# Reading split weights behind the first differential head's operands, and cutting GpSimd's two-tile operations into pieces of 256 columns

## The chip, the cores and the metric

The kernel runs on one core of a Trainium2 chip. The metric is the time of one execution on the device in microseconds (us); less is better. A core has TensorE (matmuls; PE in the profile), VectorE (DVE), ScalarE (ACT), GpSimd (POOL) and SyncE (SP), which issues all of this kernel's DMAs on one queue.

## The reference

Two layers of a decoder trunk on one sequence of 512 tokens, 1024 wide, in float32. Per layer: a half-step SwiGLU network, a mixer of three head groups, another half-step network. Cut to what matters here:

```python
for l in range(DEPTH):                                   # DEPTH = 2
    x = x + 0.5 * swiglu(rmsnorm(x, ffn1_norm[l]), ffn1_wg[l], ffn1_wu[l], ffn1_wd[l])
    h = rmsnorm(x, mix_norm[l]) @ w_in[l]                # one projection for all three groups
    h_a, h_b, h_c = jnp.split(h, [A_COLS, A_COLS + B_COLS], axis=-1)
    o_a = mla_mixer(h_a, ...)                            # 6 heads
    o_b = nsa_mixer(h_b, ...)                            # 6 heads: compressed, selected and window branches
    o_c = diff_mixer(h_c, ...)                           # 4 differential heads
    x = x + jnp.concatenate([o_a, o_b, o_c], axis=-1) @ w_out[l]
    x = x + 0.5 * swiglu(rmsnorm(x, ffn2_norm[l]), ffn2_wg[l], ffn2_wu[l], ffn2_wd[l])
return rmsnorm(x, final_norm)
```

A differential head computes two causal softmax attentions with q and k of 32 columns each and subtracts one, times a learned factor, from the other. Some columns of q and k are turned by position (rotary embedding) first.

## The kernel before

**Arithmetic.** Products are made as three passes over split numbers: each float32 operand becomes a high part (rounded on ScalarE, L162) and a low part (the difference, L164, on VectorE or GpSimd; L166 where a scale comes in). `split` makes such a pair, `mm3` and `mm3y` run the passes (0,0), (0,1), (1,0) for each k tile of 128. `SPARE` names the places whose low part GpSimd makes. Weights go through `weights`: a DMA to a `raw` tile (4 buffers), then the split into a `whl` tile of 1 MB (4 buffers).

**Split ahead.** `AHEAD` names eight column blocks of w_in. During the first network's down projection `split_ahead` splits these and stores the 1 MB pair in a DRAM array, `pre`. When the mixer comes to such a block, `weights` finds its key in `PRE` and reads the pair back (L185, `whl<-pre`) in one DMA on SyncE's queue.

**The start of the mixer.** `project2` makes column blocks 12 and 13 (q and k of the differential heads are blocks 12 to 15), `project` 14 and 15. `c_done` rotates, scales and splits each and `put` writes each half into one of two DRAM arrays, `S["C"]` (`part<-b`, L755, eight writes of 256 KB). `c_load(h)` gathers the operands of head h from them in six DMAs of 128 KB (`qk<-part`, L194). `c_load(0)` comes next, then `norm_token`, then the value projection of this group.

**Periods.** From there `PLAN` sets the order. A row names the head whose scores are made (front), the head whose weighted sum is made (back), an order string, and the items whose matmuls `period` puts between them. The first row is `("c0", "", "...f.f..f.f..f..f..", "p2 p0 cl1 cl2")`: the scores of differential head 0 with the projections of blocks 2 and 0 and the loads for heads 1 and 2. The second has head 1's scores, head 0's weighted sum, and `"lat p1 b3 cl3 an"`. `p2`, `p0`, `p1` call `project`; block 2 is `AHEAD[0]`. TensorE's order is fixed by the program there (`mm` keeps it); on the other engines a scheduler that simulates the program places each instruction. SyncE's DMAs share eight completion semaphores in turn, so an issue waits for the landing of the eighth DMA before it.

**GpSimd.** It does L164 where asked, both multiplications and the last of `rsqrt_slow` (L211, L212, L214), the second half of each rotation (L556, L557 in `rope`, L729, L730 in `roped`, L952, L953 in `a_query`) and L866, besides the squares of the norms (L298) and a few more. Up to here each of them is one instruction, over 192 to 1024 columns.

Of the kernel before, what the change touches and what calls it, by code (L numbers as in the profile page):

```python
# [14 lines left out]
ALU = mybir.AluOpType  # L15
AX = mybir.AxisListType

P = 128
# [74 lines left out]
SPARE = ('an', 'h6', 'h9', 'ho3', 'ho4', 'hq0', 'hq1', 'hq2', 'hq3', 'w0', 'w2', 'w3', 'w7')  # L93
NROW = 2

AHEAD = (2, 0, 1, 3, 9, 8, 5, 4)
# [7 lines left out]
def tile_hybrid_trunk(ctx: ExitStack, tc: tile.TileContext, I, out, dbg=None):  # L104
    nc = tc.nc
    pe, ve, sc, gp, sy = nc.tensor, nc.vector, nc.scalar, nc.gpsimd, nc.sync
# [11 lines left out]
    def nm(s):  # L118
        uid[0] += 1
        return f"{s}_{uid[0]}"  # L120
# [5 lines left out]
    def psum(tags, shape=(P, T)):  # L126
        turn[0] += 1
        tag = tags[turn[0] % len(tags)]
        return pp.tile(list(shape), F32, tag=tag, name=nm("ps" + tag), bufs=BANKS[tag])
# [6 lines left out]
    def pair(tag, dt=F32R):  # L136
        return bp.tile([P, 2, T], dt, tag=tag, name=nm(tag), bufs=PAIRS[tag])

    def tmp(dt=F32, shape=(P, T)):
        return tp.tile(list(shape), dt, tag="t", name=nm("t"), bufs=6)  # L140
# [8 lines left out]
    def loaded(src):  # L149
        t = tp.tile([P, T], F32, tag="xin", name=nm("xin"), bufs=2)  # L150
        sy.dma_start(t, src)
        return t
# [4 lines left out]
    def f32(ap):  # L157
        return ap.bitcast(F32) if ap.dtype == F32R else ap

    def split(src, hi, lo, scale=None, eng=ve):  # L160

        high = sc.copy(hi, src) if scale is None else sc.mul(hi, src, scale)  # L162
        if scale is None:
            eng.tensor_tensor(lo, src, f32(hi), op=ALU.subtract)  # L164
        else:
            eng.scalar_tensor_tensor(lo, src, scale, f32(hi), op0=ALU.mult, op1=ALU.subtract)  # L166
        return high

    def weight_tiles():
        return (wp.tile([P, 8 * P], F32, tag="raw", name=nm("raw"), bufs=RAWS),  # L170
                wp.tile([P, 2, WPAD], F32R, tag="whl", name=nm("whl"), bufs=WHLS))

    PRE = {}

    def split_ahead(src, key):

        hl = weights(src, eng=ve)
        d = PRE[key] = dp.tile([P, 2, 8 * P], F32, name=nm("pre"))
        sy.dma_start(d, f32(hl[:, :, :8 * P]))

    def weights(src, rows=P, cols=8 * P, eng=gp, key=None):

        if key in PRE:
            hl = wp.tile([P, 2, WPAD], F32R, tag="whl", name=nm("whl"), bufs=WHLS)
            sy.dma_start(f32(hl[:, :, :8 * P]), PRE.pop(key))  # L185
            return hl
        raw, hl = weight_tiles()
        sy.dma_start(raw[:rows, :cols], src)
        split(raw[:rows, :cols], hl[:rows, 0, :cols], hl[:rows, 1, :cols], eng=eng)
        return hl  # L190

    def move(dst, src):

        return sy.dma_start(f32(dst), f32(src))  # L194

    PASS = ((0, 0), (0, 1), (1, 0))
# [8 lines left out]
    def rsqrt_slow(ps, mul, r):  # L205

        ms, y = tmp(), tmp()
        sc.activation(y, ps, AF.Ln, bias=epst, scale=mul)
        sc.activation(ms, ps, AF.Identity, bias=epst, scale=mul)
        sc.activation(y, y, AF.Exp, scale=-0.5)  # L210
        gp.tensor_tensor(r, y, y, op=ALU.mult)  # L211
        gp.tensor_tensor(r, r, ms, op=ALU.mult)  # L212
        sc.activation(r, r, AF.Identity, bias=halft, scale=-0.5)
        gp.tensor_tensor(r, r, y, op=ALU.mult)  # L214
        return r

    def rsqrt(ps, mul, r):
# [117 lines left out]
    tabs = dp.tile([3, 2, P, T], F32, name="tabs")  # L335
# [29 lines left out]
    def halves_of(src):  # L365

        n = src.shape[1]
        hl = wp.tile([P, 2, WPAD], F32R, tag="whl", name=nm("whl"), bufs=WHLS)
        split(src, hl[:, 0, :n], hl[:, 1, :n])
        return hl  # L370
# [180 lines left out]
    def rope(src, cos, sin, swap, r0=0, r1=P, eng=gp):  # L551

        t, sw = tmp()[r0:r1], tmp()[r0:r1]
        ve.stream_shuffle(sw, src, swap)
        ve.tensor_tensor(t, src, cos[r0:r1], op=ALU.mult)
        eng.tensor_tensor(sw, sw, sin[r0:r1], op=ALU.mult)  # L556
        eng.tensor_tensor(t, t, sw, op=ALU.add)  # L557
        return t

    def mm(*args, **kw):  # L560
# [3 lines left out]
    def mm3y(ps, pairs):  # L564

        n = len(pairs)
        for k, (w, x) in enumerate(pairs):
            for j, (a, b) in enumerate(PASS):
                mm(ps, w(a), x(b), start=k == j == 0, stop=k == n - 1 and j == 2)
                yield  # L570
# [101 lines left out]
    def mix(l, xn, nxt):  # L672
# [4 lines left out]
        S = {}  # L677
# [15 lines left out]

        def project(c, done, eng=gp):

            w = weights(I["w_in"][l, c], eng=ve if "w%d" % c in SPARE else eng, key=("in", l, c))
            pj = psum("m")
            yield from mm3y(pj, [((lambda a, k=k: w[:, a, k * P:(k + 1) * P]), (lambda b, k=k: xg[k][:, b])) for k in range(KD)])
            done(pj)
# [18 lines left out]
        def scaled(pj, by):  # L718
            t = tmp()
            ve.tensor_tensor(t, pj, by, op=ALU.mult)  # L720
            return t

        def roped(pj, g, swap, n=P, eng=gp):

            t = scaled(pj, rs[0])
            c, sw = tmp()[:n], tmp()[:n]
            ve.stream_shuffle(sw, t[:n], swap)
            ve.tensor_tensor(c, t[:n], loaded(tabs[g, 0])[:n], op=ALU.mult)
            eng.tensor_tensor(sw, sw, loaded(tabs[g, 1])[:n], op=ALU.mult)  # L729
            eng.tensor_tensor(t[:n], c, sw, op=ALU.add)  # L730
            return t

        def scales(n):
# [3 lines left out]
        def halves(t, scale=None, eng=ve):  # L737
            hl = btile()
            n = t.shape[0]
            split(t, hl[:n, 0], hl[:n, 1], scale, eng)  # L740
            return hl
# [65 lines left out]
        def c_load(h):  # L807

            qk = S["cqk", h] = [pair("qk"), pair("qk")]
            for c in range(2):  # L810
                src = S["C"][c].rearrange("j (d h m) n -> j d h (m n)", h=4, m=2)[:, :, h]
                dst = qk[c].rearrange("p m n -> p (m n)")
                for j in range(3):
                    move(dst[32 * j:32 * j + 32], src[PASS[j][1 - c]])

        def c_front(h):
            qk = S["cqk", h]
# [43 lines left out]
        def a_query1(pj):  # L861
            mg = S["mg"]
            t = S["at1"] = scaled(pj, rs[0])
            q = tmp()
            sc.activation(q[:64], t[:64], AF.Square)
            gp.tensor_tensor(S["aq0"][:64], S["aq0"][:64], q[:64], op=ALU.add)  # L866
            ca1 = S["ca1"] = halves(t[:64], mg[:64, 1:2])

            kp = rope(t[64:96], loaded(tabs[0, 0]), loaded(tabs[0, 1]), SWAP16, 64, 96)
            split(kp, ca1[64:96, 0], ca1[64:96, 1])  # L870
# [38 lines left out]
        def a_weights(a):  # L909

            if ("wa", a) not in S:
                S["wa", a] = weights(I["w_a%d" % a][l], cols=(640, 768, 512)[a], eng=ve if "wa%d" % a in SPARE else gp)
            return S["wa", a]
# [28 lines left out]
        def a_query(h):  # L942
            a, s = h // 2, h % 2
            w, ca0, ca1, ta = a_weights(a), S["ca0"], S["ca1"], S["ta"]
            q = S["aq", h] = pair("qk")
            pj = psum("m")
            yield from mm3y(pj[:96], [((lambda c: w[:, c, 96 * s:96 * s + 96]), (lambda b: ca0[:, b])),
                                      ((lambda c: w[:64, c, 192 + 96 * s:192 + 96 * s + 96]), (lambda b: ca1[:64, b]))])
            t, sw = tmp(), tmp()
            ve.tensor_tensor(t[:96], pj[:96], ta[:96, 0], op=ALU.mult)  # L950
            ve.stream_shuffle(sw[64:96], pj[64:96], SWAP16)  # L951
            gp.tensor_tensor(sw[64:96], sw[64:96], ta[64:96, 1], op=ALU.mult)  # L952
            gp.tensor_tensor(t[64:96], t[64:96], sw[64:96], op=ALU.add)  # L953
            split(t[:96], q[:96, 0], q[:96, 1], eng=gp if "hq%d" % h in SPARE else ve)

        def a_front(h):
# [18 lines left out]
        def b_rope(c):  # L975
            def done(pj):
                t = roped(pj, 1, SWAP16, P if c == 3 else 64) if c in (3, 6) else scaled(pj, rs[0])
                scale = {3: scales(1), 8: scales(2), 4: B_SCALE, 5: B_SCALE}.get(c)
                t = halves(t, scale, gp if "h%d" % c in SPARE else ve)
                for r, n, p, at in B_PIECES[c]:  # L980
                    if ("part", p) not in S:
                        S["part", p] = parts(3 * P if p == "q" else P)
                    put(S["part", p], at, t, r, n)
            return project(c, done)
# [165 lines left out]
        for c in (C_TOP + 2, C_TOP + 3):  # L1150
            for _ in project(c, c_done(c, ve), ve):
                pass
# [155 lines left out]
```

## Time and profile before

| | us |
|---|---|
| median of 3 runs | 2020.51 (2019.13 to 2026.75) |
| the profiled execution, its time | 2023.87 |
| its span | 2022.1 |
| TensorE busy | 1968.2 (97%) |
| VectorE busy | 1473.4 (73%) |
| ScalarE busy | 1066.5 (53%) |
| GpSimd busy | 253.5 (13%), 183 instructions |

The mean granted clock of TensorE is 0.99 of its full 2.4 GHz. Layer 0's mixer begins near 360 us of the span, layer 1's near 1357. A busy TensorE need not run at its peak, and time in which an engine idles costs only where TensorE's chain goes through it; so the chain, TensorE's waits and the clock in the windows are to be read together.

### The profile page before, as it was taken

What the parts mean: (1) busy time and instruction counts of PE and PEld (TensorE: products, weight loads), DVE (VectorE), ACT (ScalarE), POOL (GpSimd) and SP (SyncE); (2) the same over time, 40 slices, a digit from 0 to 9 for tenths busy, and PEclk for the clock granted to TensorE, in tenths of its full rate; (3) what the DMA queues carried; (4) which work ended last, traced back from release to release, by engine and by line L of the source; (5) the groups of instructions that cost most, each with busy time, mean ns of one, the idle gap of its engine ahead of it and who ended that gap; (6) DMA issues with size and microseconds to landing.
All of it is one profiled execution on the core that took longest, in us unless ns stands there. A gap on an engine that the chain in (4) does not pass through costs nothing.

```text
span 2022.1 us, 31129 instructions
## 1 busy us (share of the span) xinstructions
PE 1968.2 (97%) x11864; PEld 1711.7 (85%) x11864; DVE 1473.4 (73%) x2315; ACT 1066.5 (53%) x2010; POOL 253.5 (13%) x183
## 2 busy tenths in 40 slices
PE   8999999989999999999999999999989999999997
PEld 6899988867777899998889999887668778999886
DVE  8888874478887888883378887444898878888623
ACT  4455643266687545562255556333667764555521
POOL 5000001025420100001100000110354010000011
PEclk9999999999999999999999999999999999999999
DMA  6333388664632523334442335777447143333431
GB/s 209 105 105 105 114 282 266 207 213 129 179 105 81 170 94 105 105 118 138 131 143 88 106 107 170 245 230 228 158 135 214 53 146 115 95 106 106 133 114 55
DMA packets 104549, 288.46 MB, mean 143 GB/s; under 512 B 14928, under 2 KB 18768, under 8 KB 104400
## 3 DMA queue, kind: packets, MB, share of 16 engines
q1 hardware_dynamic: 104400, 286.48, 45.5%
q8 instruction: 93, 1.52, 0.3%
q14 instruction: 56, 0.46, 0.1%
HBM read 237.77 MB, written 46.66 MB: 141 GB/s over the span
## 4 chain that ended last, share of the span: by engine, by line
PE 83%; DVE 8%; DMA 2%; ACT 2%; issue 2%; SPq 1%; POOL 1%; DVEq 0%; ACTq 0%; POOLq 0%
PE psm L562 19%; PE psm L203 14%; PE pss L562 11%; PE pst L203 10%; PE pst L562 9%; PE pss L203 8%; PE pso L562 6%; PE pso L203 5%; PE pst L573 1%; DVE nmx L595 1%; DVE pt L164 1%; DMA part<-b 1%; DVE b L166 1%; DMA qk<-part 1%; SPq L194 1%
## 5 line engine op out<-in xcount | busy, mean ns | idle before, releaser
L162 ACT CAST whl<-raw 128x1024 fp32r<-128x1024 f32 (+2 forms) x417 | 383.8, 923 | 489.8 <-issue 104.8
L164 DVE TENSOR_TENSOR whl<-raw,whl 128x1024 fp32r<-128x1024 f32 (+2 forms) x383 | 420.1, 1099 | 222.2 <-ACT whl L162 221.4
L562 PE MATMUL psm<-b,whl 128*128 128x256 f32 (+1 forms) x2140 | 448.6, 346 | 3.6 <-DVE t L951 3.6
L562 PEld LDWEIGHTS psm<-b,whl 128*128 128x128 f32 x2140 | 328.8, 192 | 44.5 <-issue 8.0
L203 PE MATMUL psm<-b,whl 128*128 128x512 f32 (+1 forms) x948 | 230.6, 383 | 1.2 <-DVE whl L164 1.0
L298 POOL TENSOR_TENSOR t<-t,t 128x512 f32<-128x512 f32 x48 | 78.3, 1632 | 1104.2 <-ACT t L292 777.4
L203 PEld LDWEIGHTS psm<-b,whl 128*128 128x128 f32 x948 | 174.7, 189 | 36.5 <-DVE whl L164 1.4
L203 PE MATMUL pst<-b,whl 128*128 128x512 f32 x624 | 158.6, 394 | 3.0 <-DVE b L166 1.2
L203 PEld LDWEIGHTS pst<-b,whl 128*128 128x128 f32 x624 | 117.3, 189 | 31.3 <-DVE b L166 3.1
L596 ACT ACTIVATE pn<-pss,nmx 128x256 f32<-128x256 f32 x208 | 109.6, 528 | 64.6 <-DVE nmx L595 63.3
L595 DVE TENSOR_REDUCE nmx<-pss 128x1 f32<-128x256 f32 x208 | 97.7, 485 | 42.2 <-PE pss L562 30.9
L203 PE MATMUL pss<-b,whl 128*128 128x512 f32 x504 | 126.3, 390 | 0.0
L562 PE MATMUL psm<-qk,whl 128*128 128x256 f32 x840 | 123.7, 284 | 0.0
L562 PE MATMUL pst<-b,whl 128*128 128x256 f32 (+1 forms) x816 | 121.2, 290 | 0.2 <-DVE b L164 0.2
L562 PE MATMUL pss<-b,whl 128*128 128x256 f32 (+1 forms) x816 | 120.8, 290 | 0.0
L562 PEld LDWEIGHTS psm<-qk,whl 128*128 128x128 f32 x840 | 111.2, 192 | 0.3
L203 PEld LDWEIGHTS pss<-b,whl 128*128 128x128 f32 x504 | 94.7, 188 | 19.5
L562 PEld LDWEIGHTS pst<-b,whl 128*128 128x128 f32 x816 | 108.5, 192 | 2.9 <-DVE b L164 0.5
L562 PEld LDWEIGHTS pss<-b,whl 128*128 128x128 f32 x816 | 108.9, 192 | 2.1
L164 DVE TENSOR_TENSOR whl<-pn,whl 128x1024 fp32r<-128x1024 f32 x63 | 77.2, 1226 | 26.2 <-ACT whl L162 26.2
L562 PE MATMUL pst<-qk,whl 128*128 128x256 f32 x576 | 84.8, 284 | 0.0
L562 PE MATMUL pss<-qk,whl 128*128 128x256 f32 x576 | 84.8, 283 | 0.0
(314 smaller groups left out, 3402.6 us busy)
## 6 DMA issues: line engine op xcount, KB each, us to landing
raw<-in_ffn_gu_dram SPq DMA_DIRECT2D x174, 512.0 KB, 3.7
raw<-in_ffn_d_dram SPq DMA_DIRECT2D x64, 512.0 KB, 3.7
pre<-whl SPq DMA_DIRECT2D x16, 1024.0 KB, 5.5
whl<-pre SPq DMA_DIRECT2D x16, 1024.0 KB, 7.0
raw<-in_w_in_dram SPq DMA_DIRECT2D x28, 512.0 KB, 6.0
raw<-in_ffn_d_dram SPq DMA_DIRECT2D x32, 384.0 KB, 3.4
xin<-xs SPq DMA_DIRECT2D x48, 256.0 KB, 3.0
raw<-in_w_out_dram SPq DMA_DIRECT2D x32, 256.0 KB, 2.8
```

What stands on the lines that cost most here:

```text
L162: high = sc.copy(hi, src) if scale is None else sc.mul(hi, src, scale)
L164: eng.tensor_tensor(lo, src, f32(hi), op=ALU.subtract)
L166: eng.scalar_tensor_tensor(lo, src, scale, f32(hi), op0=ALU.mult, op1=ALU.subtract)
L194: return sy.dma_start(f32(dst), f32(src))
L203: pe.matmul(ps, w(a), x(b), start=first and k == 0 and j == 0, stop=last and k == n - 1 and j == 2)
L298: gp.tensor_tensor(sq, sq, self.acc, op=ALU.add)
L562: return tc.keep_in_program_order(pe.matmul(*args, **kw))
L573: return tc.keep_in_program_order(pe.transpose(dst, src, idn))
L595: ve.reduce_max(nmx, part[i], axis=AX.X, negate=True)
L596: sc.activation(pn[i], part[i], AF.Exp, bias=nmx, accum_out=sm[:, i:i + 1])
```

## The change

One part is in `project` and `weights`: the read of a `pre` array may be placed behind another instruction. For every block but `AHEAD[0]` it is placed behind the last of the six reads of the layer's first `c_load`, `S["cl0"]`. The other part is a helper, `pieces`, which cuts a two-tile operation of GpSimd on a 2-D tile into pieces of 256 columns; on other engines it leaves one instruction. L298, L296, L294, L326 and the 3-D operations L1078 and L1079 are not cut. GpSimd has 116 more instructions, 58 a layer.

```diff
+    def pieces(eng, o, a, b, op):
+
+        n = o.shape[1]
+        m = P * 2 if eng is gp and len(o.shape) == 2 else n
+        for c in range(0, n, m):
+            d = min(c + m, n)
+            eng.tensor_tensor(o[:, c:d], a[:, c:d], b[:, c:d], op=op)
+
     def split(src, hi, lo, scale=None, eng=ve):
...
-            eng.tensor_tensor(lo, src, f32(hi), op=ALU.subtract)
+            pieces(eng, lo, src, f32(hi), op=ALU.subtract)
...
-    def weights(src, rows=P, cols=8 * P, eng=gp, key=None):
+    def weights(src, rows=P, cols=8 * P, eng=gp, key=None, behind=None):
 
         if key in PRE:
             hl = wp.tile([P, 2, WPAD], F32R, tag="whl", name=nm("whl"), bufs=WHLS)
-            sy.dma_start(f32(hl[:, :, :8 * P]), PRE.pop(key))
+            with tc.issue_after(behind.ins) if behind else ExitStack():
+                sy.dma_start(f32(hl[:, :, :8 * P]), PRE.pop(key))
             return hl
...
-        gp.tensor_tensor(r, y, y, op=ALU.mult)
-        gp.tensor_tensor(r, r, ms, op=ALU.mult)
+        pieces(gp, r, y, y, op=ALU.mult)
+        pieces(gp, r, r, ms, op=ALU.mult)
         sc.activation(r, r, AF.Identity, bias=halft, scale=-0.5)
-        gp.tensor_tensor(r, r, y, op=ALU.mult)
+        pieces(gp, r, r, y, op=ALU.mult)
...
-            w = weights(I["w_in"][l, c], eng=ve if "w%d" % c in SPARE else eng, key=("in", l, c))
+            w = weights(I["w_in"][l, c], eng=ve if "w%d" % c in SPARE else eng, key=("in", l, c),
+                        behind=S.get("cl0") if c != AHEAD[0] else None)
...
                 for j in range(3):
-                    move(dst[32 * j:32 * j + 32], src[PASS[j][1 - c]])
+                    done = move(dst[32 * j:32 * j + 32], src[PASS[j][1 - c]])
+            S.setdefault("cl0", done)
```

The pairs of GpSimd operations in `rope`, `roped` and `a_query` and the one at L866 become calls of `pieces` in the same way.

SyncE's queue at the start of layer 0's mixer, before: `whl_3845` is block 0 (p0), the parts are the last two pairs of writes, the first two groups of `qk` are head 0's operands.

```order
L755 DMA part_3535<-b_3605 64x2x512
L755 DMA part_3536<-b_3605 64x2x512
L185 DMA whl_3845<-pre_2808 128x2x1024
L755 DMA part_3535<-b_3642 64x2x512
L755 DMA part_3536<-b_3642 64x2x512
L194 DMA qk_3647<-part_3535 32x1024 x3
L194 DMA qk_3648<-part_3536 32x1024 x3
L194 DMA qk_3914<-part_3535 32x1024 x3
```

The same place now:

```order
L765 DMA part_3535<-b_3605 64x2x512
L765 DMA part_3536<-b_3605 64x2x512
L765 DMA part_3535<-b_3642 64x2x512
L765 DMA part_3536<-b_3642 64x2x512
L203 DMA qk_3647<-part_3535 32x1024 x3
L203 DMA qk_3648<-part_3536 32x1024 x3
L194 DMA whl_3845<-pre_2808 128x2x1024
L203 DMA qk_3914<-part_3535 32x1024 x3
```

Block 0's read moved behind the last two part writes and head 0's six reads; head 1's and head 2's twelve reads follow it, then the reads of blocks 1 and 3. Layer 1 has the same move. TensorE's order is unchanged.

VectorE in the period of differential head 2, before: `t_4130` is what GpSimd's L214 leaves, `pt` and `pt_615` are splits of turned probabilities.

```order
L595 TENSOR_REDUCE nmx_4237<-pss_4234 128x1
L878 TENSOR_SCALAR b_4140<-t_4130 64x512
L880 SCALAR_TENSOR_TENSOR b_4140<-xin_4142,t_4130 32x512
L880 SCALAR_TENSOR_TENSOR b_4140<-xin_4145,t_4130 32x512
L164 TENSOR_TENSOR pt_4247<-pst_4242,pt_4247 128x512
L164 TENSOR_TENSOR pt_615_4253<-pst_4250,pt_615_4253 128x256
```

The same place now:

```order
L604 TENSOR_REDUCE nmx_4245<-pss_4242 128x1
L166 TENSOR_TENSOR pt_4255<-pst_4250,pt_4255 128x512
L166 TENSOR_TENSOR pt_615_4261<-pst_4258,pt_615_4261 128x256
L889 TENSOR_SCALAR b_4148<-t_4135 64x512
L891 SCALAR_TENSOR_TENSOR b_4148<-xin_4150,t_4135 32x512
L891 SCALAR_TENSOR_TENSOR b_4148<-xin_4153,t_4135 32x512
```

The two splits moved ahead of the three operations that need GpSimd's result.

GpSimd just ahead of that, now:

```order
L166 TENSOR_TENSOR t_4105<-t_4105,xin_4110 128x256 x2
L166 TENSOR_TENSOR t_4135<-t_4137 128x256 x2
L166 TENSOR_TENSOR t_4102<-t_4104,t_4105 128x256 x2
L166 TENSOR_TENSOR t_4135<-t_4135,t_4136 128x256 x2
L166 TENSOR_TENSOR t_4135<-t_4135,t_4137 128x256 x2
```

These were five instructions of 512 columns in the same order; all pieces carry the line of the helper, L166.

## Rows read from the trace of the kernel before

**Rows 1.** The page, chain of the work that ended last, share of the span by engine.

```profile
PE 83%; DVE 8%; DMA 2%; ACT 2%; issue 2%; SPq 1%; POOL 1%; DVEq 0%; ACTq 0%; POOLq 0%
```

**Rows 2.** TensorE's waits over the whole span: what waited, for what; us in total, times, longest.

```profile
PE pss L562 <- ACT pn L596: 9.8, 19, 1.8
PE pst L573 <- DVE pt L164: 8.3, 10, 2.3
PE pss L562 <- DMA qk<-part: 6.1, 2, 4.0
...
PE pso L562 <- DVE pt L164: 3.2, 5, 1.0
```

**Rows 3.** Windows (from:to in us): length, busy time (instructions) of PE, PEld, DVE, ACT, POOL, then TensorE's granted clock, DMA share, GB/s. The first two lie right behind the waits for `qk<-part`, the others are one and the same stretch of work in layer 0 and in layer 1.

```profile
401.80:405.20 3.40, 3.40 (x12) 2.51 (x12) 1.53 (x4) 1.67 (x6) 0.00 (x0) 0.50 1.02 236
1400.20:1405.30 5.10, 5.10 (x15) 3.92 (x16) 1.54 (x4) 1.69 (x6) 0.00 (x0) 0.50 1.04 235
...
472.10:541.90 69.80, 63.33 (x368) 50.26 (x367) 60.41 (x114) 45.52 (x113) 36.43 (x24) 0.95 0.57 155
1471.70:1539.30 67.60, 62.50 (x368) 49.71 (x367) 60.26 (x113) 45.65 (x112) 36.28 (x23) 0.95 0.56 154
```

**Rows 4.** Timeline of TensorE at the start of the first period, layer 0, then layer 1: start, us, what. `pss<-qk,qk` is head 0's first score, the x3 `psm` (one of them is still p2's, the other two are p0's) is where p0 begins, the x1 `psm` is where p1 begins.

```profile
401.54 0.42 PE L562 MATMUL pss<-qk,qk 96*128 96x256 f32 x2 [2.12 <-DMA qk<-part]
...
406.60 0.95 PE L562 MATMUL psm<-b,whl 128*128 128x512 f32 x3
...
414.23 0.79 PE L562 MATMUL psm<-b,whl 128*128 128x512 f32 x1
...
1400.17 0.66 PE L562 MATMUL pss<-qk,qk 96*128 96x256 f32 x2 [3.97 <-DMA qk<-part]
...
1406.05 0.94 PE L562 MATMUL psm<-b,whl 128*128 128x512 f32 x3
...
1413.69 0.79 PE L562 MATMUL psm<-b,whl 128*128 128x512 f32 x1
```

**Rows 5.** Timeline of SyncE's queue in layer 0, then layer 1: when DMAs are issued, and how long the issuing takes (of all in a row).

```profile
386.81 0.56 SPq L185 DMA_DIRECT2D whl<-pre  x1
387.46 2.15 SPq L755 DMA_DIRECT2D part<-b  x2
395.71 8.23 SPq L194 DMA_DIRECT2D qk<-part  x18
...
1384.02 0.58 SPq L185 DMA_DIRECT2D whl<-pre  x1
```

**Rows 6.** DMAs by the time of issue, narrow windows, in this order: the part write at 385.95, block 0's read at 386.81, the part write at 387.46, the operand reads near 397.96, the reads of blocks 1 and 3 at 404.13 and 404.80; in layer 1 block 0's read at 1384.02 and the part write behind it. The last column is us from issue to landing.

```profile
part<-b SPq DMA_DIRECT2D x1, 256.0 KB, 4.9
whl<-pre SPq DMA_DIRECT2D x1, 1024.0 KB, 8.1
part<-b SPq DMA_DIRECT2D x1, 256.0 KB, 8.1
qk<-part SPq DMA_DIRECT2D x2, 128.0 KB, 3.3
whl<-pre SPq DMA_DIRECT2D x1, 1024.0 KB, 7.1
whl<-pre SPq DMA_DIRECT2D x1, 1024.0 KB, 10.8
...
whl<-pre SPq DMA_DIRECT2D x1, 1024.0 KB, 9.3
part<-b SPq DMA_DIRECT2D x1, 256.0 KB, 9.3
```

**Rows 7.** The chain of work that ended last, in order of time (start, us, what): the same pieces in layer 0 and in layer 1, and one of GpSimd in layer 0.

```profile
367.57 17.05 PE psm L562 x75
...
472.10 1.87 DVE sm L825
...
512.24 2.77 POOL t L729
...
1364.37 17.05 PE psm L562 x75
...
1471.69 1.88 DVE sm L825
```

**Rows 8.** GpSimd's groups by line and form: us in total, mean ns of one, then the idle time before them.

```profile
L164 POOL TENSOR_TENSOR whl<-raw,whl 128x1024 fp32r<-128x1024 f32 x10 | 24.8, 2478 | 6.7 <-ACT whl L162 6.2
L164 POOL TENSOR_TENSOR whl<-raw,whl 128x512 fp32r<-128x512 f32 x18 | 24.5, 1360 | 73.0 <-ACT whl L162 73.0
...
L326 POOL TENSOR_TENSOR pn<-b,rstd 128x256 f32<-128x256 f32 x6 | 4.9, 849 | 15.1 <-DVE rstd L226 15.1
```

**Rows 9.** Timelines of VectorE and of GpSimd: start, us, what, and the idle time before it with what ended it.

```profile
430.63 0.23 DVE L825 TENSOR_SCALAR sm<-sm,nlam 128x4 f32<-128x4 f32 x1
445.40 0.42 DVE L878 TENSOR_SCALAR b<-t 64x512 f32<-64x512 f32 x1 [1.22 <-POOL t L214]
471.54 2.40 POOL L164 TENSOR_TENSOR whl<-raw,whl 128x1024 fp32r<-128x1024 f32 x1
2006.34 0.42 DVE L225 TENSOR_TENSOR rstd<-rstd,t 128x256 f32<-128x256 f32 x1
2007.26 3.60 DVE L328 SCALAR_TENSOR_TENSOR pn<-b,gains,rstd 128x256 f32<-128x256 f32 x5
2007.30 2.48 POOL L326 TENSOR_TENSOR pn<-b,rstd 128x256 f32<-128x256 f32 x3 [9.87 <-DVE rstd L226]
```

More of the change, by code (lines that the diff above doesn't have):

```diff
@@ L555, in rope @@
         ve.tensor_tensor(t, src, cos[r0:r1], op=ALU.mult)
-        eng.tensor_tensor(sw, sw, sin[r0:r1], op=ALU.mult)
-        eng.tensor_tensor(t, t, sw, op=ALU.add)
+        pieces(eng, sw, sw, sin[r0:r1], op=ALU.mult)
+        pieces(eng, t, t, sw, op=ALU.add)
         return t
@@ L728, in roped @@
             ve.tensor_tensor(c, t[:n], loaded(tabs[g, 0])[:n], op=ALU.mult)
-            eng.tensor_tensor(sw, sw, loaded(tabs[g, 1])[:n], op=ALU.mult)
-            eng.tensor_tensor(t[:n], c, sw, op=ALU.add)
+            pieces(eng, sw, sw, loaded(tabs[g, 1])[:n], op=ALU.mult)
+            pieces(eng, t[:n], c, sw, op=ALU.add)
             return t
@@ L865, in a_query1 @@
             sc.activation(q[:64], t[:64], AF.Square)
-            gp.tensor_tensor(S["aq0"][:64], S["aq0"][:64], q[:64], op=ALU.add)
+            pieces(gp, S["aq0"][:64], S["aq0"][:64], q[:64], op=ALU.add)
             ca1 = S["ca1"] = halves(t[:64], mg[:64, 1:2])
@@ L951, in a_query @@
             ve.stream_shuffle(sw[64:96], pj[64:96], SWAP16)
-            gp.tensor_tensor(sw[64:96], sw[64:96], ta[64:96, 1], op=ALU.mult)
-            gp.tensor_tensor(t[64:96], t[64:96], sw[64:96], op=ALU.add)
+            pieces(gp, sw[64:96], sw[64:96], ta[64:96, 1], op=ALU.mult)
+            pieces(gp, t[64:96], t[64:96], sw[64:96], op=ALU.add)
             split(t[:96], q[:96, 0], q[:96, 1], eng=gp if "hq%d" % h in SPARE else ve)
```

## The prediction

> **What bounds the kernel now.** I read the chain of work first: TensorE is 83% of it, VectorE 8%, DMA 2%, GpSimd 1% [rows 1]. An edit pays where TensorE stands still or runs at its lower clock. The list of TensorE's waits comes second: the longest single ones are the two for the operands of differential head 0, `qk<-part`, one in each layer, 6.1 us together; waits behind VectorE's pt splits and ScalarE's exponentials make another 8.3 + 3.2 and 9.8 us, none longer than 2.3 [rows 2]. Third, the windows: right behind each of the two waits the granted clock is 0.50, the 1.2 GHz level, for 3.40 us in layer 0 and 5.10 us in layer 1, with TensorE busy in all of it [rows 3]. Layer 0's wait ends at 401.54 and began 2.12 us before, so TensorE was ready at 399.42; in layer 1 it ends at 1400.17 after 3.97, ready at 1396.20 [rows 4].
>
> Why the operands are late is in SyncE's queue. The 1 MB read whl<-pre (column block 0) is issued at 386.81, the last two part writes behind it at 387.46 [rows 5]. The part write ahead of that read lands 4.9 us after its issue, the one behind it needs 8.1; in layer 1 read and write both take 9.3 [rows 6]. The reads of the operands wait for the last part and start at 395.71 [rows 5].
>
> **The change part by part.** *The moved read.* Its own issue (0.56 us [rows 5]) moves past two part writes and six operand reads; nothing else on the path moves on SyncE. The last two part writes then take the place at 386.8 and about 0.9 later. With the 4.9 us of the write that had no 1 MB ahead of it they land near 391.7 and 392.6; in layer 1 (start 1384.0) near 1388.9 and 1389.8. The 18 reads took 8.23 us to issue, 0.46 each [rows 5]. Three of the six need only the first array, so the last is issued some 1.3 us behind the second write's landing and lands 3.3 us later [rows 6]: 397.2 and 1394.4. TensorE is ready at 399.42 and 1396.20, so both waits go, with 2.2 and 1.8 us to spare: 6.1 us. Without the stop I expect no fall of the clock behind it; work done at half clock takes half the time, 3.40/2 + 5.10/2 = 4.25 us. Gross gain 10.3 us. If only the wait went and the clock fell all the same it would be 6.1.
>
> *What is late next.* The read of block 0 is now issued near 394.4 (1391.6). The nearest rows are the reads at 404.13 and after: 7.1 us for the first of a pair, 10.8 for the second [rows 6]. It stands alone among operand reads, as the first did, so I take 7.0: 401.4 and 1398.6. Its user p0 starts 406.60 - 401.54 = 5.06 us after the first score in layer 0 and 1406.05 - 1400.17 = 5.88 in layer 1 [rows 4], of which 1.70 and 2.55 were lost to the clock: needed at 402.8 and 1399.5. Covered, by 1.4 and 0.9 us. Then the read for p1: an issue waits for the landing of the eighth before it, so five of the twelve following operand reads, and p1's weights behind them, wait for block 0; they go out about 2.5 us after it lands, 403.9 and 1401.1, and land after 7.0 at 410.9 and 1408.1. Needed, by the same way (414.23 and 1413.69, 12.69 and 13.52 behind the first score, less the clock [rows 4]), at 410.4 and 1407.2. Late by 0.5 and 0.9: a cost of 1.4 us, between 0 (if the transfers are faster because nothing stood still ahead of them) and 3. Net gain of the move 8.9 us.
>
> *Does it last?* Between the layers there is a natural trial. The stretch before the wait starts 996.80 us apart (367.57, 1364.37), VectorE's L825 at 472.10 and 1471.69 is 999.59 apart [rows 7]: 2.8 us, which is what layer 1 lost more here (1.85 of waiting, 0.85 of clock). Lateness goes one to one through 70 us in which VectorE has much of the chain. But the next stretch, the same work, takes 69.80 us in layer 0 and 67.60 in layer 1, though the granted clock is 0.95 in both [rows 3]. Part of that is a GpSimd operation of 2.77 us on layer 0's chain [rows 7], so I read it as other luck, not as slack, and keep the low end for it.
>
> *The pieces.* 116 more GpSimd instructions, 58 a layer. Whole ones take 2478 ns (1024 columns), 1360 (512) and 849 (256) [rows 8]. Four of 849 against 2478 is 0.31 us for each piece added, two against 1360 is 0.34; the slope of the larger two, 2.18 ns a column, leaves 0.24. So 28 to 39 us more GpSimd time in all. GpSimd is on 1% of the chain, 20 us or some 15 operations of 1.3 us: one extra piece each costs 4 to 5 us at the most, and I take 3. Against it stands the stop of VectorE beside a long GpSimd instruction: L825 on four columns takes 0.23 us at 430.63 and 1.87 at 472.10 [rows 7, 9], where GpSimd's 2.40 us split runs [rows 9]. A piece would let it in after 0.85 at the most, about 1 us sooner; that place stands on the chain in both layers [rows 7], and with one more like it I take 3 us. The reverse shows too: at 2007.26, beside three GpSimd pieces of 256, five VectorE operations take 3.60 us, 0.72 each, where one alone takes 0.42 [rows 9]. Cost and relief cancel. Cutting also changes the order on VectorE: the scalings L878 and L880, which keep VectorE idle for 1.22 us on the result of L214 [rows 9], now stand behind two pt splits that were ready. That wait goes in both layers: 2.4 us, between 0 (if the splits arrive later than L214's last piece) and 2.4; I take 2.
>
> On those stops the Trainium skill has a rule, in "SBUF — State Buffer", section "Who interferes with whom": of VectorE and GpSimd, whoever issues first holds the ports that they share for its whole instruction, and the other blocks fully, whatever the shape. By that rule alone every stop ends with its piece and the sum would be rival 2, 2002.5; it says nothing for cutting as such, since VectorE's instructions can then hold up the pieces in turn. The 1.87 us agree with it; the alternation at 2007.26 is why I don't follow it to the end.
>
> *Sum.* Gain 8.9 + 2.0 + 0 = 10.9 us. The profiled execution has a span of 2022.1 and a time of 2023.87, so it would be 2013.0; it lies 3.36 above the median of the runs, 2020.51, from which the same 10.9 gives 2009.6. All times below are on the median's scale.
>
> **The rivals.** (1) *The weights become the wait; slower.* If the reads of block 0 and of p1 take L us instead of 7.0, p0 waits L - 8.4 and p1 lands at 396.9 + 2L against 410.4: together 2L - 13.5, and a stop of a few us brings its own 2 us of half clock. The gain of 5.2 a layer is used up from L = 8.4 on. For it: the read took 8.1 and 9.3 where it is now, 10.8 as second of a pair [rows 6]; a transfer share of 1.02 of the DMA engines in the window at 401.80 [rows 3]. Against: those stood behind or beside other 1 MB of traffic, and 7.1 is the row with the same neighbours. At L = 10.8 each layer loses 8.1 + 4.2, and with the other terms the sum is 24.6 - 10.3 - 2.0 = 12.3 slower, 2032.8. Chance 0.07. (2) *The pieces free VectorE.* Waits behind splits and exponentials (8.3 + 9.8 + 3.2 us [rows 2]) shrink by a third, 7 us more: 2002.5. For it the 1.87 us row; against it that TensorE's waits come mostly at other places. Chance 0.18. (3) *The pieces cost.* GpSimd's 15 operations on the chain each get their piece (5 us) and VectorE alternates with pieces at 0.72 instead of 0.42 in a dozen places (4 us), without relief: 2009.6 + 3 to 9, about 2016, no change by the bound. Chance 0.16. (4) *Half of the move is given back*, because p1 is 3 us late or the clock falls at a later gap: 2014.5, no change. Chance 0.09. That the change does nothing is excluded by the order: both reads stand behind the operands there, TensorE's order is the same.
>
> **How the numbers follow.** The forecast, 2009.6 with 2005 to 2014, has 0.50. Half a per cent, about what a measurement here can tell from no change, is 10.1 us: the bound lies at 2010.4. Of the forecast 0.31 lies below it; with rival 2 that is 0.49 faster. Slower is rival 1, 0.07. The rest, 0.44, is within. The range leaves out rival 1 and the ends of rivals 2 and 3: 2001 to 2019.
>
> **What would show it.** In the changed profile: the wait `qk<-part` gone from TensorE's list, or under 1 us; no window at 0.50 between the first score and p0; the last part writes landing about 5 us after their issue. Block 0 landing ahead of p0's first matmul, a gap under 1 us ahead of p1's. GpSimd's busy time up by 28 to 39 us, L825 at 472 near 0.9. I am wrong if a wait on whl<-pre stands in the place of the old one, if the half-clock stretches move to p1, or if GpSimd's lines on the chain grow by more than 5 us.

## The result and the profile after

The changed kernel takes 2012.01 us, median of 5 runs (2010.47 to 2012.74). Against 5 runs of the kernel before (median 2026.02) the ratio is 0.9938, 95% interval 0.9922 to 0.9955: 12.6 us faster, between 9 and 16. The forecast was 10.9 us; its 2009.6 counts from 2020.51, the median of the three runs at hand then. In the comparisons below the kernel before has medians from 2023.98 to 2026.28, so gains are compared here and not times. The profiled execution has a span of 2009.7 us, 12.4 less than before.

The page of the changed kernel, first part (busy time, share, instructions), then its chain by engine, which answers to [rows 1]:

```profile
PE 1963.7 (98%) x11864; PEld 1709.4 (85%) x11864; DVE 1463.1 (73%) x2315; ACT 1066.5 (53%) x2010; POOL 279.3 (14%) x299
...
PE 87%; DVE 7%; ACT 3%; POOL 2%; issue 1%; DMA 1%; SPq 0%; DVEq 0%; ACTq 0%; POOLq 0%
```

GpSimd is busy for 25.8 us more, VectorE for 10.3 us less with as many instructions, 2315. DMA's share of the chain falls from 2% to 1%, GpSimd's rises from 1% to 2%. TensorE's waits in the changed kernel answer to [rows 2]:

```profile
PE pst L582 <- DVE pt L166: 7.8, 10, 2.1
PE pss L571 <- ACT pn L605: 7.3, 15, 1.3
PE psm L571 <- DVE t L962: 6.6, 2, 3.7
...
PE pso L571 <- DVE pt L166: 1.5, 3, 0.6
...
PE psm L571 <- DMA whl<-pre: 0.9, 1, 0.9
```

The two waits for `qk<-part` are gone, the waits for ScalarE and for the pt splits 4.7 us shorter. Two entries are worse: a wait for a read of split weights (0.9), and the two for L962, 6.6 instead of 3.6.

The moved read, in SyncE's timeline of the changed kernel, layer 0, against [rows 5]:

```profile
384.49 2.52 SPq L765 DMA_DIRECT2D part<-b  x3
390.72 2.70 SPq L203 DMA_DIRECT2D qk<-part  x6
393.46 0.57 SPq L194 DMA_DIRECT2D whl<-pre  x1
394.07 10.07 SPq L203 DMA_DIRECT2D qk<-part  x12
404.24 1.69 SPq L194 DMA_DIRECT2D whl<-pre  x2
```

and its DMAs by the time of issue (the last part write at 386.24, block 0's read at 393.46 and, in layer 1, at 1386.72, the read for p1 at 404.24; last column us to landing), against [rows 6]:

```profile
part<-b SPq DMA_DIRECT2D x1, 256.0 KB, 5.0
whl<-pre SPq DMA_DIRECT2D x1, 1024.0 KB, 8.4
whl<-pre SPq DMA_DIRECT2D x1, 1024.0 KB, 6.7
whl<-pre SPq DMA_DIRECT2D x1, 1024.0 KB, 6.5
```

The last part write lands 5.0 us after its issue instead of 8.1, the reads of the operands start at 390.72 instead of 395.71. TensorE's timeline of the changed kernel at the first period, layer 0 and then layer 1, and the windows right behind the first score (columns as in [rows 3]), against [rows 3, 4]:

```profile
397.53 0.34 PE L571 MATMUL pss<-qk,qk 96*128 96x256 f32 x2
...
402.00 0.70 PE L571 MATMUL psm<-b,whl 128*128 128x512 f32 x2 [0.55 <-DVE nmx L604]
...
410.84 0.47 PE L571 MATMUL psm<-b,whl 128*128 128x512 f32 x1 [0.88 <-DMA whl<-pre]
...
1391.99 0.34 PE L571 MATMUL pss<-qk,qk 96*128 96x256 f32 x2
```

```profile
397.50:400.90 3.40, 3.40 (x18) 2.50 (x16) 1.44 (x4) 1.90 (x7) 0.00 (x0) 1.00 1.05 282
1392.00:1397.10 5.10, 5.10 (x28) 4.00 (x27) 2.87 (x7) 2.58 (x10) 0.00 (x0) 1.00 1.06 254
...
474.00:480.80 6.80, 6.52 (x26) 5.53 (x26) 4.03 (x10) 3.40 (x11) 0.00 (x0) 0.50 0.67 180
511.50:518.30 6.80, 6.80 (x35) 5.47 (x35) 4.97 (x11) 3.30 (x8) 6.49 (x10) 0.50 0.76 195
637.80:641.20 3.40, 3.40 (x10) 2.61 (x9) 0.18 (x1) 0.00 (x0) 0.00 (x0) 0.50 0.00 0
1501.40:1508.20 6.80, 6.72 (x27) 4.70 (x28) 6.22 (x14) 3.61 (x9) 6.40 (x10) 0.50 0.68 191
```

The first score comes without a wait, at the full 2.4 GHz in both layers; 18 and 28 matmuls run in the stretch where 12 and 15 ran before. Half clock is still there, elsewhere: behind the wait for a pt split at 474, near the mixer's end, and behind both waits for L962 (before 511 and 1501).

Since TensorE's order is the same in all these kernels, its instructions can be laid side by side. The table gives by how many us an instruction starts earlier than in the kernel before, at the time in the first row (start before minus start now, each of one profiled execution). The first column is the start of the program, ahead of the moved read. The move alone is the same program as the kernel before up to there and has 1.1, so differences of some 1 us are scatter between executions. The row with zeros is experiment 7, its added matmuls left out.

| us before | 399.0 | 405.1 | 439.3 | 478.2 | 522.8 | 646.1 | 1395.1 | 1405.8 | 1438.7 | 1485.4 | 1519.7 | 2012.1 |
|---|---|---|---|---|---|---|---|---|---|---|---|---|
| changed | 1.7 | 5.6 | 5.6 | 7.9 | 4.8 | 4.1 | 4.1 | 10.6 | 11.4 | 14.1 | 11.6 | 12.4 |
| move alone | 1.1 | 5.0 | 5.0 | 4.4 | 3.3 | 2.6 | 2.6 | 9.1 | 9.1 | 6.2 | 6.9 | 6.3 |
| move, zeros | -0.1 | 3.8 | 3.8 | 3.8 | 3.9 | 4.7 | 4.7 | 11.2 | 11.2 | 9.9 | 9.7 | 9.8 |
| pieces alone | 1.2 | 0.4 | 0.5 | 2.8 | 2.4 | 3.3 | 3.3 | 5.8 | 6.5 | 9.2 | 6.8 | 6.9 |
| move, 8 pieces | 0.9 | 4.8 | 4.9 | 6.4 | 6.7 | 7.5 | 7.5 | 14.0 | 14.3 | 14.4 | 16.0 | 12.8 |
| pieces of 128 | -1.7 | 2.1 | 2.8 | 5.0 | 5.0 | 7.0 | 7.0 | 13.6 | 14.8 | 18.6 | 17.7 | 19.0 |
| 128, splits whole | 0.5 | 4.4 | 4.5 | 2.6 | -0.9 | -1.7 | -1.7 | 4.8 | 5.8 | 1.8 | -0.2 | -0.4 |

At its place the move is worth 3.84 us in layer 0 and 6.57 in layer 1, in the changed kernel and alone. What differs is what comes behind it.

### The profile page after: what moved, and what is told of

Same layout as the page of the kernel before. It is cut to its first block, busy times and chain, and to the rows that moved or that the text cites. A ratio compares the mean times of both kernels' runs of the same rounds, so it can differ in the third digit from the quotient of the medians.

```text
span 2009.7 us, 31247 instructions
## 1 busy us (share of the span) xinstructions
PE 1963.7 (98%) x11864; PEld 1709.4 (85%) x11864; DVE 1463.1 (73%) x2315; ACT 1066.5 (53%) x2010; POOL 279.3 (14%) x299
## 4 chain that ended last, share of the span: by engine, by line
PE 87%; DVE 7%; ACT 3%; POOL 2%; issue 1%; DMA 1%; SPq 0%; DVEq 0%; ACTq 0%; POOLq 0%
PE psm L571 22%; PE psm L212 14%; PE pss L571 11%; PE pst L212 9%; PE pst L571 9%; PE pss L212 8%; PE pso L571 6%; PE pso L212 5%; PE pst L582 1%; DVE nmx L604 1%; DVE pt L166 1%; ACT pn L605 1%; DVE pn L839 1%; POOL t L307 1%; DVE pn L649 1%
## 5 line engine op out<-in xcount | busy, mean ns | idle before, releaser
L166 DVE TENSOR_TENSOR whl<-raw,whl 128x1024 fp32r<-128x1024 f32 (+2 forms) x383 | 420.7, 1101 | 222.2 <-ACT whl L170 221.4
L307 POOL TENSOR_TENSOR t<-t,t 128x512 f32<-128x512 f32 x48 | 78.9, 1644 | 1104.1 <-ACT t L301 790.4
L604 DVE TENSOR_REDUCE nmx<-pss 128x1 f32<-128x256 f32 x208 | 97.4, 484 | 35.3 <-PE pss L571 24.7
L166 DVE TENSOR_TENSOR whl<-pn,whl 128x1024 fp32r<-128x1024 f32 x63 | 77.2, 1225 | 26.3 <-ACT whl L170 26.3
L166 POOL TENSOR_TENSOR whl<-raw,whl 128x256 fp32r<-128x256 f32 (+2 forms) x90 | 72.1, 826 | 171.7 <-ACT whl L170 169.0
```

Of the source, the lines that this page charges most:

```text
L166: eng.tensor_tensor(o[:, c:d], a[:, c:d], b[:, c:d], op=op)
L307: gp.tensor_tensor(sq, sq, self.acc, op=ALU.add)
L604: ve.reduce_max(nmx, part[i], axis=AX.X, negate=True)
```

## The experiments

Ratios are to the kernel before on the same chip, with 95% intervals; us are worked out from the ratio and some 2024 us.

**1. The move alone.**

```diff
-        m = P * 2 if eng is gp and len(o.shape) == 2 else n
+        m = n
```

> The moved read alone, GpSimd's operations whole. SyncE's order differs from the kernel before only in block 0's read, the other engines' orders not at all. Theory (the read's move carries the gain): both waits for qk<-part gone, about 9 us faster, ratio near 0.9955, between 0.993 and 0.997. Rival (the pieces carry it, by freeing VectorE and changing its order): 3 to 6 us, ratio 0.997 to 0.9985, because the wait for block 0's weights takes back a part.

Measured: 2018.07 us, 0.9973 (0.9964 to 0.9982), 5.5 us faster (3.6 to 7.3). Outside what the theory said and inside the rival's range, but not for the rival's reason: the longest wait for block weights is 1.0 us. Both waits and the half clock behind them are gone (10.4 us in the table), and half of that is lost again: between 439 and 646 us in layer 0, between 1438 and 1485 in layer 1. These two stretches in the kernel before, then in the move alone, with the same 1140 and 222 matmuls (columns as in [rows 3]):

```profile
439.30:646.10 206.80, 193.09 (x1140) 150.91 (x1141) 176.94 (x367) 146.21 (x380) 65.88 (x48) 0.98 0.41 121
1438.70:1485.40 46.70, 43.21 (x222) 32.88 (x223) 41.00 (x74) 32.69 (x78) 19.68 (x13) 0.96 0.56 165
```

```profile
434.20:643.50 209.30, 197.09 (x1140) 153.83 (x1141) 176.88 (x367) 146.55 (x380) 65.92 (x48) 0.96 0.40 119
1429.60:1479.20 49.60, 45.89 (x222) 35.30 (x223) 41.73 (x75) 33.03 (x78) 19.61 (x13) 0.90 0.54 160
```

They are 2.5 and 2.9 us longer. TensorE is busy in them for 4.0 and 2.7 us more, at a lower granted clock, and idle for 1.5 us less and 0.2 more. So what is lost is clock; the waits there are in sum not longer. TensorE's timeline and the windows of this kernel at the second of these places, and the same place of the kernel before in both layers:

```profile
1429.59 0.49 PE L571 MATMUL pss<-qk,qk 96*128 96x512 f32 x1 [1.80 <-ACT pn L605]
```

```profile
434.40:437.80 3.40, 3.40 (x13) 2.80 (x14) 1.96 (x4) 2.25 (x5) 1.53 (x2) 0.50 0.12 45
...
1431.10:1437.90 6.80, 6.29 (x20) 4.49 (x19) 5.28 (x11) 5.05 (x14) 1.46 (x2) 0.50 0.32 77
```

```profile
439.27 0.50 PE L562 MATMUL pss<-qk,qk 96*128 96x512 f32 x1 [1.82 <-ACT pn L596]
...
1438.73 0.49 PE L562 MATMUL pss<-qk,qk 96*128 96x512 f32 x1 [1.81 <-ACT pn L596]
```

```profile
438.50:442.00 3.50, 2.47 (x14) 1.76 (x14) 2.75 (x7) 2.78 (x7) 2.48 (x3) 1.00 0.33 102
...
1439.50:1442.90 3.40, 3.39 (x12) 2.33 (x9) 2.88 (x6) 2.95 (x8) 0.92 (x1) 0.50 0.00 0
```

The wait is the same 1.8 us in all four (1.83 in the move alone in layer 0). Behind it the kernel before ran at 1.00 in layer 0 and at 0.50 for 3.4 us in layer 1, the move alone at 0.50 in both, for 3.4 and 6.8 us.

**2. The pieces alone.**

```diff
-                        behind=S.get("cl0") if c != AHEAD[0] else None)
+                        behind=None)
```

> The pieces alone, block 0's read where it was. VectorE's and ScalarE's orders are those of the changed kernel. Theory: the two waits for qk<-part stay (about 6 us together, half clock behind them); 2 to 4 us faster, ratio 0.998 to 0.999. Rival (pieces carry it): 7 us or more, ratio under 0.9965.

Measured: 2018.93 us, 0.9979 (0.9969 to 0.9989), 4.3 us (2.2 to 6.3), just past the theory's upper end. The waits for `qk<-part` stay, 5.8 us. So on top of the pieces the move is worth 12.6 - 4.3 = 8.3 us by the ratios, with an error of some 4, and on the kernel before 5.5. The difference is not shown: by the profiled executions the move is worth 2015.1 - 2009.7 = 5.4 us on top of the pieces and 2022.1 - 2015.8 = 6.3 on the kernel before. Busy times of the move alone and of the pieces alone, from their pages:

```profile
PE 1968.6 (98%) x11864; PEld 1712.8 (85%) x11864; DVE 1472.4 (73%) x2315; ACT 1066.6 (53%) x2010; POOL 253.1 (13%) x183
PE 1963.6 (97%) x11864; PEld 1708.1 (85%) x11864; DVE 1464.7 (73%) x2315; ACT 1065.7 (53%) x2010; POOL 279.6 (14%) x299
```

TensorE's busy time changes by 0.4 us with the move on the kernel before (1968.2) and by 0.1 on top of the pieces (to 1963.7); the rest is idle time, 6.7 and 5.5 us. Over the whole span, in these four executions, the move saves the waiting and nothing of the clock.

**3 and 4. The move with pieces in one sort of place.** First in the low parts of splits only (the first edit, and the same in the other calls outside `split`), then everywhere but there (the second edit).

```diff
-        pieces(gp, r, y, y, op=ALU.mult)
+        gp.tensor_tensor(r, y, y, op=ALU.mult)
```

```diff
-            pieces(eng, lo, src, f32(hi), op=ALU.subtract)
+            eng.tensor_tensor(lo, src, f32(hi), op=ALU.subtract)
```

> The moved read, and pieces only in the low parts of splits (72 more GpSimd instructions); rotations and rsqrt_slow whole. VectorE's order is then that of the kernel before. If what the pieces bring comes from the changed order, this is as fast as the move alone, within 0.1%. If it comes from shorter stops of VectorE beside the long split instructions, it is 2 us or more faster than the move alone.

> The moved read, and pieces only in rotations, rsqrt_slow and L866 (44 more GpSimd instructions); splits whole. VectorE's order is nearly that of the changed kernel. If the changed order brings it, this is as fast as the changed kernel, within 0.1%; if the splits' pieces do, it is as fast as the move alone.

Measured: 2013.54 us, 0.9952 (0.9938 to 0.9966), and 2014.37 us, 0.9960 (0.9945 to 0.9974). Splits in pieces bring 4 us on the move alone with VectorE's order unchanged, by intervals that just overlap; the others bring 2.7 with the changed order, inside the error, and lie between both theories. That the whole needs both sorts is not shown: both intervals overlap the changed kernel's.

**5. The move and 8 pieces.** Only GpSimd's two operations in `roped` are cut, in two each, 8 more instructions in all; every other call of `pieces` is one instruction again, as in

```diff
-            pieces(eng, lo, src, f32(hi), op=ALU.subtract)
+            eng.tensor_tensor(lo, src, f32(hi), op=ALU.subtract)
...
-        pieces(gp, r, y, y, op=ALU.mult)
+        gp.tensor_tensor(r, y, y, op=ALU.mult)
```

> The moved read, and pieces only in the rotation of roped (8 more GpSimd instructions in all). That is enough for the scheduler to give VectorE most of the changed kernel's order (the three scalings behind the two pt splits, the four scalings of probabilities later). If the order brings what rotations' pieces brought, about 2.5 us less than the move alone, ratio near 0.996, and TensorE gains 2 to 3 us on the move alone between 439 and 470 us in each layer. If the shortness of the pieces brings it: as the move alone, 0.997 to 0.998.

Measured: 2011.16 us, 0.9929 (0.9915 to 0.9943), 14 us. As fast as the changed kernel with 116 pieces; more than the theory said. TensorE gains 2.1 us on the move alone between 439 and 478 in layer 0 (table), as expected; the rest is that in this execution less is lost from 478 to 646 and from 1439 to 1485. Experiment 4 has these 8 pieces and 36 more, and is slower by 3 us by the medians, 6 by the ratios; why is open.

**6. Splits of weights whole, all other pieces kept.**

```diff
-        split(raw[:rows, :cols], hl[:rows, 0, :cols], hl[:rows, 1, :cols], eng=eng)
+        split(raw[:rows, :cols], hl[:rows, 0, :cols], hl[:rows, 1, :cols], eng=eng, whole=True)
```

> The changed kernel with GpSimd's splits of weights whole again (56 fewer instructions), all other pieces kept. If pieces beside VectorE's short operations bring the gain through the weights' splits, 2 to 4 us slower than the changed kernel, ratio 0.995 to 0.996. If their price on GpSimd's chain (four pieces of a weight split and four pieces of a rotation take 6.5 us at 1486 us of layer 1, and VectorE waits behind them) is larger, 1 to 2 us faster than the changed kernel, ratio 0.993 or less, and the wait of 3.7 us for L962 is back near 1.8.

Measured: 2010.27 us, 0.9925 (0.9911 to 0.9939). As fast as the changed kernel, within the error, and the waits for L962 are back at 3.6 us together, as the second theory said. So these 56 pieces bring nothing here that the error lets show. Their price stands in the changed kernel's chain, layer 1 (start, us, what):

```profile
1485.92 3.10 POOL whl L166 x3
1489.02 0.07 issue
1489.09 3.37 POOL t L166 x4
```

Three of four pieces of a weight split and four of a rotation stand in the chain ahead of ScalarE and VectorE; TensorE's wait of 3.7 us at 1501.48 is the end of it.

**7. The move and a filled wait.** Seven matmuls of zeros in front of the wait of experiment 1, ahead of the third score tile of head 2. They add zeros to the projection that `mm3y` is summing (`live`).

```diff
+            if tiles[0] == NT - 1:
+                warm(keep)
             bank = psum("s")
```

```python
def warm(n):
    ps = live[0]
    for _ in range(n if ps is not None else 0):
        mm(ps, zero[:, :ps.shape[0]], zero[:, :ps.shape[1]], start=False, stop=False, skip_group_check=True)
```

> The moved read alone, and seven matmuls of zeros (added into the projection that is being summed, about 1.5 us) ahead of the third score tile of differential head 2, where TensorE otherwise waits 1.8 us in each layer and a stretch at half clock follows. Theory (half of the move's gain goes back in stretches at half clock behind later waits): the stretches near 434 and 431 us vanish, 2 to 3 us faster than the move alone, ratio 0.996. Rival (VectorE and ScalarE set the end there, the clock costs nothing): no change against the move alone, 0.9973.

Measured: 2016.50 us, 0.9955 (0.9942 to 0.9968), 3.6 us less than the move alone by the ratios, whose intervals just overlap, and 1.6 by the medians. The trace has 14 such matmuls, seven in each layer. TensorE's timeline and the window:

```profile
433.49 1.69 PE L571 MATMUL psm<-zero 128*128 128x512 bf16 x7
435.47 0.50 PE L571 MATMUL pss<-qk,qk 96*128 96x512 f32 x1 [0.30 <-ACT pn L617]
```

```profile
430.00:437.00 7.00, 6.70 (x38) 4.65 (x39) 6.14 (x12) 4.12 (x11) 4.87 (x4) 1.00 0.78 245
1422.00:1432.00 10.00, 8.45 (x45) 5.75 (x46) 8.80 (x18) 7.04 (x18) 5.04 (x4) 1.00 0.60 183
```

No half clock is left there in either layer. By the table 0.9 us are gained between 439 and 646, where the move alone loses 2.4, and 1.3 are lost between 1438 and 1485 instead of 2.9. So a part of the move's gain went into the clock at this place; that the whole kernel is faster for it is likely, but its error leaves it open.

**8, 10 and 12. Pieces of 128 columns:** everywhere, everywhere but in splits (with the second edit of 3 and 4), in splits only (with the first).

```diff
-        m = P * 2 if eng is gp and len(o.shape) == 2 else n
+        m = P if eng is gp and len(o.shape) == 2 else n
```

> The changed kernel with pieces of 128 columns (208 more GpSimd instructions than with 256). If shorter stops of VectorE are what the pieces bring, it is as fast as the changed kernel or 1 to 2 us faster; if the price of an instruction on GpSimd's chain, 0.24 to 0.34 us, decides, 3 to 8 us slower, ratio 0.9955 to 0.998, with GpSimd 50 to 70 us longer busy.

> Pieces of 128 columns in all places but the low parts of splits, which are whole (192 fewer GpSimd instructions than with 128 everywhere). VectorE's order is nearly that of the kernel with 128 everywhere. If the order makes that kernel fast: 0.989 to 0.991. If short pieces beside VectorE's operations do: 0.992 or more, between it and the kernel with 8 pieces.

> The counterpart of the run with 128 columns outside splits: the moved read, pieces of 128 columns in the low parts of splits only, all else whole; VectorE's order is nearly that of the kernel before (12 lines differ, against 112 with 128 everywhere). If short pieces free VectorE beside long splits whatever its order, clearly faster than the move alone and than pieces of 256 in splits: 0.991 to 0.994. If the kernel with 128 everywhere owes its time to its order together with short splits, no more than with 256 in splits: 0.995 to 0.9965.

Measured: 2003.98 us, 0.9894 (0.9880 to 0.9908), 21 us: the fastest of all, faster than either theory said, with GpSimd at 317.9 us. Without pieces in splits: 2021.06 us, 0.9982 (0.9972 to 0.9992), no faster than the move alone, though VectorE's order is nearly that of 128 everywhere (18 lines differ). With pieces in splits only: 2012.09 us, 0.9936 (0.9922 to 0.9951), VectorE's order nearly that of the kernel before; clearly faster than the move alone, as the first theory said, but not clearly faster than with pieces of 256 in splits (experiment 3). So in these runs the order that the scheduler makes for 128 columns is good only with short splits. A reason can be seen at one place, VectorE's four L839 (the difference of the two softmaxes) in layer 0, beside GpSimd. With whole splits (experiment 10), timelines of both:

```profile
468.40 7.19 DVE L839 SCALAR_TENSOR_TENSOR pn<-pn,sm,pn 128x128 f32<-128x128 f32 x4
...
468.01 2.73 POOL L172 TENSOR_TENSOR whl<-raw,whl 128x1024 fp32r<-128x1024 f32 x1
470.70 1.34 POOL L172 TENSOR_TENSOR qk<-t,qk 96x512 fp32r<-96x512 f32 x1
472.52 2.52 POOL L172 TENSOR_TENSOR whl<-raw,whl 128x1024 fp32r<-128x1024 f32 x1 [0.49 <-ACT whl L170]
```

With 128 everywhere (experiment 8):

```profile
468.76 2.76 DVE L839 SCALAR_TENSOR_TENSOR pn<-pn,sm,pn 128x128 f32<-128x128 f32 x4
...
469.71 4.22 POOL L166 TENSOR_TENSOR whl<-raw,whl 128x128 fp32r<-128x128 f32 x8
```

The same four take 3.87 us in the changed kernel and 1.93 in the move alone, where a split ran beside only the last of them. With whole splits TensorE waits 5.6 us for L839 (`PE pst <- DVE pn`), in the move alone 1.0. All 32 of them in experiment 10, ns, shortest, median, longest:

```profile
L839 DVE SCALAR_TENSOR_TENSOR pn<-pn,sm,pn x32: 339/671/2824, 413.5 to 1470.9; 128x128 f32<-128x128 f32 x8, 128x256 f32<-128x256 f32 x8, 128x384 f32<-128x384 f32 x8, 128x512 f32<-128x512 f32 x8
```

The longest is 2824 here, 1225 with pieces of 256, 947 with 128, 753 in the move alone. The rule of the Trainium skill that the prediction weighed ("SBUF — State Buffer", "Who interferes with whom") has a VectorE instruction with two inputs in SBUF contend with a GpSimd instruction that reads SBUF. These rows agree with it: the 2824 ns stand beside GpSimd's split at 472.52, while the third of the four, which started at 472.24 with GpSimd idle, took 607.

**9. The order by hand, no piece.** L878 and L880 are written as an item of their own.

```diff
-    ("c2", "c1", "ff....fbf..f.bb..f.bb...", "t9 ak0 av0"),
+    ("c2", "c1", "ff....fbf..f.bb..f.bb...", "t9 ta ak0 av0"),
...
+        def a_table():
+            rq = S["rq"]
+            ta = S["ta"] = btile(F32)
+            ve.tensor_scalar(ta[0:64, 0], rq[0:64], A_SCALE, None, op0=ALU.mult)
...
```

> The moved read, no piece at all; the three scalings L878 and L880 are written as an item of their own in the period of differential head 2, behind t9, so that VectorE has the two pt splits ahead of them as in the changed kernel. TensorE's order and GpSimd's operations are those of the move alone. If the order is what the pieces bring, as fast as the run with 8 pieces and as the changed kernel, 0.9925 to 0.9945. If the pieces themselves are needed: as the move alone, 0.997.

Measured: 2016.17 us, 0.9961 (0.9948 to 0.9975): 2.4 us on the move alone, inside its error, and clearly slower than with 8 pieces. This agrees with the 2 us that the prediction gave the three scalings but does not show them, since VectorE's order differs from the move alone's at some 45 places here. What the 8 pieces bring beyond this is not settled: their order differs from this one's at some 30 places (probabilities' scalings, splits of keys, compressed blocks of layer 0).

**11. Pieces of 128, without the move.** The edit of experiment 2 on top of that of experiment 8.

> Pieces of 128 columns everywhere, block 0's read where it was; all orders but SyncE's are those of the run with 128 and the move. If the move's gain of 10 us at its place is given back only where later waits bring stretches at half clock, it is worth more here, where such waits are shorter: 8 to 11 us, ratio 0.993 to 0.995. If it is worth 5 us as on the kernel before: 0.9915 to 0.9925.

Measured: 2010.82 us, 0.9933 (0.9919 to 0.9946). The move is worth 21.5 - 13.6 = 7.9 us here by the ratios, with an error of some 4, and 2007.8 - 2003.1 = 4.7 by the profiled executions. The ratio lies in the first theory's range and its interval reaches into the second's, so this does not decide between them. TensorE is busy for 2.0 us less with the move here (1963.2 to 1961.2) and idle for 2.7 less, so in this pair a part of the clock's gain did stay.

## Why the prediction was right, and where not

**The moved read, at its place: right in mechanism and size.** 6.1 us of waiting and 4.25 of half clock were forecast, 10.3 together; 3.84 + 6.57 = 10.4 were measured, and the last part write landed in 5.0 us where 4.9 was taken (layer 0).

**What is late next: right in sum, not in place.** Block 0's read took 8.4 us in layer 0 and 6.7 in layer 1, where 7.0 was taken for both. It landed at 401.87, and p0's first matmul followed at 402.00 after 0.55 us (the profile names VectorE's L604, which reads a score that this matmul does not use; its weight load waits for the read's landing). So block 0 did not land ahead of p0, one of the prediction's signs. p1 waited 0.88. That is 1.4 us, all in layer 0, where 0.5 and 0.9 were forecast, one in each layer. It cost nothing in the end: at 439 the lead is 5.6 us, as it was at 405. Rival 1 had the whole gain of a layer used up at a read of 8.4 us, and it was 8.4 here: its price was too high, since p1's read took 6.5 and no half clock followed.

**"Does it last?": the step that failed.** One to one was forecast, from the distance of the layers, with the later loss of layer 0 put down to luck. The move alone kept 5.5 us of 10.4. The waiting that it saved stayed saved; the clock's 4.25 us were lost again to half clock behind later waits, as rival 4 had it with a chance of 0.09. That is the prediction's own lower case, 6.1 us, only at other places than the one it named. In the natural trial the stretch behind, 69.80 us against 67.60 [rows 3], had taken back 2.2 of the 2.8 us; that was read and set aside. Whether it keeps more on top of the pieces, where the 1.8 us wait is 1.3 and no half clock follows it, is open: 8.3 us by the ratios, 5.4 by the profiled executions. Why the same wait is followed by half clock in one execution or layer and not in the other is not shown either.

**The pieces: under-sized.** 2 us were forecast, of order, with cost and relief cancelling; 4.3 were measured alone and 7 on top of the move, by the profiled executions 7 and 6. At 472 they do cancel: in the move alone L836, the two L174 and the four L839 take 1.87 + 1.84 + 0.68 + 1.93 = 6.3 us, in the changed kernel 0.21 + 1.26 + 1.22 + 3.87 = 6.6. The forecast's 0.9 for L836 came out as 0.21. Over the whole span VectorE is busy for 10 us less, so the relief is larger than the two places that were counted. The alternation was priced from 0.72 against 0.42 of another operation; a scalar_tensor_tensor like those five, over the same 256 columns, takes 0.48 in the move alone with GpSimd idle. GpSimd's added time, 25.8 us, lies under the forecast's 28 to 39. Its share of the chain rose from 1% to 2%, by 19 us, which is past the 5 us named as a sign of being wrong; more than half of its time there is in the norms' squares, L305 and L307, which aren't cut, so the sign says little of the pieces. Of the order, the 1.22 us of idle time ahead of L878 is gone, in the changed kernel's timeline of VectorE:

```profile
438.93 1.02 DVE L166 TENSOR_TENSOR pt<-pst,pt 128x512 fp32r<-128x512 f32 x2 [0.28 <-ACT pt L170]
439.94 0.42 DVE L889 TENSOR_SCALAR b<-t 64x512 f32<-64x512 f32 x1
```

Rival 3 is real at one place, the 3 us of longer waits for L962; rival 2 over all is the stronger of the two, and with 128 columns more so. How much of the pieces' gain is order and how much shorter stops is open.

So the total, 10.9 against 12.6, came out by luck in part: counted with the move first, too much was kept of the move (8.9 against 5.5) and too little given to the pieces (2 against 7), and the two errors cancel.

## What to carry to other kernels

Book the waiting and the clock of a removed wait apart: here the waiting stayed saved, while the clock's part came back as half clock behind later waits. Read the stretches behind it for waits after which the clock has fallen, in any layer, before the gain is booked in full. Long GpSimd instructions beside a busy VectorE are a hazard that the schedule may or may not hit: cut those that run beside work on the path, and look at where a cut one is itself on the path. Where a scheduler sets the order, a cut of a few instructions can move the time as much as all of them, so compare the orders before crediting the instructions; here the two could not be told apart.

## What was not expected of the hardware

The same wait of 1.8 us of TensorE was followed by the 1.2 GHz level in one layer and not in the other of one execution. And with seven matmuls of zeros in such a wait no half clock followed it in either layer, though the kernel's gain from it is not clear of the error.
